# Moving tiles of a matmul kernel laid in a row and read in turns from neighbouring 16-byte lines

## The chip, the cores and the metric

The kernel runs on one core of a Trainium2 chip. The metric is the device time of one execution in microseconds (us). TensorE is called PE here (its weight loads PEld), VectorE DVE, ScalarE ACT, GpSimd POOL, and SyncE, which issues nearly all DMAs, SP.

## What is computed

One encoder layer on 1024 tokens of width 1024, all in float32: a SwiGLU block, a sub-layer that mixes tokens in two branches (retention and multi-scale pooling), a second SwiGLU block, and a last norm.

```python
h = x
h = h + 0.5 * swiglu_ffn(rmsnorm(h, norm_ffn1), ffn1_w_in, ffn1_w_out)      # D_FF 2816
u = rmsnorm(h, norm_mix)
q, k, v, g_ret, p, gates = jnp.split(u @ w_in, split_points, axis=-1)       # 7168 columns
q, k = rotary(q), rotary(k) * 256 ** -0.5                                   # 4 heads of 256
ret = retention(q, k, v)                  # chunks of 64 tokens, decay by head
ret = per_head_rms_norm(ret) * silu(g_ret)
pool_out = multiscale_pool(p, pool_w, pool_scale)   # windows of 2, 4, 8, 16 tokens
gate = sigmoid(gates + gate_bias)
merged = gate[0] * (ret @ w_ret_up) + gate[1] * (pool_out @ w_pool_up)
h = h + merged @ w_out
h = h + 0.5 * swiglu_ffn(rmsnorm(h, norm_ffn2), ffn2_w_in, ffn2_w_out)
out = rmsnorm(h, norm_final)
```

## The kernel before

**Matmuls.** Activations stand with features on the 128 partitions and tokens along the row. Each float32 operand is split in two parts, hi (rounded to the matmul's 32-bit type) and lo (what is left): `split` is a cast on ACT, written to hi, and a subtraction on DVE, written to lo (`split_scaled` does it with a factor). A product of two operands takes three matmuls, `mm3` (lines 203 to 205): hi by hi, hi by lo, lo by hi. One operand is stationary (128 x 128, loaded by PEld), the other moves past it, 512 columns at a time, and the sum stands in one of eight PSUM banks. A moving tile is made by `operand` (or `put`, in class `Next`, for the normed input of a stage), and a stationary one by `weights`.

**Stages.** Every large product is a Strassen-like scheme of seven half-size products. The input of a stage is recombined into the tiles R11, R12, R21, R22 and T1 to T4 (names n1, n2, ru, mg, n3 for the five stages that use `Next`), and the weights into L11, L12, S1 to S4. `strassen` accumulates a group's products in three banks (a, b, e), which ACT and DVE read out. `common` shares products of the last kind between two groups; its matmuls have 256 columns. The order of the stages: `ffn_in` (tiles a_), `ffn_out` (tiles b), the values `values` (tiles v), the other projections `project` (q, k, g, p, and t for the gates), retention with the pool's products between its steps (`Unit`, `pool`, `pool_up`), the branch projection (ru) and output projection (wo), then `ffn_in` again (c_) and `ffn_out` again (d). The last half of the second `ffn_out` makes the products with L22 with the weights moving (`near`, `far`), so that those outputs come by token.

**Order.** A Python generator gives steps (a preparation and a body); the body is run four steps later. Side work waits in a queue (`flow`) of which one or two pieces are placed after each step. A scheduler then sets each engine's order, and each engine works through its own in that order. Buffers come from pools with a fixed count: 28 tiles of 4 KB a partition (`mv`) for moving tiles, 9 (`t4`), 8 half-size ones (`c2`), and so on. A tile in such a pool can be written once the last reader of the one that had the buffer is done, a DMA to memory included.

**The moving tile's layout.** This is what the change is about. The tile holds even tokens and odd tokens apart, each with hi and lo, and the matmul reads it alternately from the two, so that the product's columns are in the order of the tokens:

```python
def rows(name):
    return sb.tile([P, 2, 2, HD], F32R, tag="mv", bufs=N_MV, name=name)   # parity, hi/lo, 256
def by_two(src):
    return src.rearrange("p (a b) -> p b a", b=2)      # every second element of the source
def moving(m, at=slice(None)):
    return [m[:, :, z, at].rearrange("p b a -> p a b") for z in range(2)]
```

Successive reads of a matmul are therefore 2 KB apart, to and fro, and the split that fills a tile reads its source with a step of two elements. The retention's tiles are not laid so (`straight`, read from start to end), nor are the operands of the small matmuls that spread a row over the partitions (n10b, n20b, fin0b).

Places in the program that the prediction uses: the square sums of a norm (`square`, ACT line 291, added on DVE line 292); the read-outs b, v, p7 in `strassen` (lines 514, 519, 536); the read-outs bd and dd in `ffn_out` (line 986) and the sums bacc, dacc (line 983); vp and vf, the read-outs in `values` (lines 1358, 1364); the gates (line 1227); fin0sum and fin0b, the statistics of the last norm.

Of the kernel before, what the change touches and what calls it, by code (L numbers as in the profile page):

```python
# [17 lines left out]
P = 128  # L18
# [72 lines left out]
def block_kernel(ctx: ExitStack, tc, x, x_tok, vecs, f1_in, f1_out, w_in, w_v, pool_w, w_ret, w_pool, w_o,  # L91
                 f2_in, f2_out, g_row, rope, decay, consts, out, out_tok):
# [29 lines left out]

    def moving(m, at=slice(None)):

        return [m[:, :, z, at].rearrange("p b a -> p a b") for z in range(2)]
# [43 lines left out]
    QUARTER = slice(0, P), slice(P, HD)  # L169
# [37 lines left out]
    def parts(m, at=slice(None)):  # L207
        return m[:, 0, at], m[:, 1, at]

# [66 lines left out]
    class Norm:  # L276


        def __init__(self, name):
            self.name, self.ssq, self.seen = name, None, set()  # L280

        def square(self, mt, tokens, src):
# [3 lines left out]
            if tokens.start not in self.seen:  # L286
                act(dst, src, AF.Square)
                self.seen.update(range(tokens.start, tokens.stop, HD))
            else:
                q = c2(f"{self.name}q{mt}_{tokens.start}")[:, : tokens.stop - tokens.start]  # L290
                act(q, src, AF.Square)
                tt(dst, dst, q, ADD)

    class Next(Norm):


# [13 lines left out]
        def put(self, n, i, src, by=None):  # L310
            m = rows(f"{self.name}{n}{i}")
            self.M[n, i] = m
            if by is None:
                split(lay(m, 0), lay(m, 1), by_two(src))
            else:
                split_scaled(lay(m, 0), lay(m, 1), by_two(src), by)
# [66 lines left out]
        def blocks(self, R, tags, over=False):  # L383
# [6 lines left out]
            def sums(z):  # L390
                for i in range(2):
                    m = self.M[R, 2 * i + z]
                    v = c2(f"{self.name}x{i}{z}").rearrange("p (b a) -> p b a", b=2)
                    tt(v, lay(m, 0).bitcast(F32), lay(m, 1).bitcast(F32), ADD)
                    x.update({(i, j, z): v[:, :, QUARTER[j]] for j in range(2)})

            def difference(n, z):
# [5 lines left out]
                if n not in left:  # L403
                    m, at = self.M[R, z], QUARTER[1]
                else:
                    tag, bufs = left[n]
                    if (R, n) not in self.made:

                        self.made[R, n] = sb.tile([P, 2, 2, HD], F32R, tag=tag, bufs=bufs, name=f"{self.name}{R}{n}")
                    m, at = self.made[R, n], QUARTER[z]  # L410
                self.Y[R, n, z] = moving(m, at)
                split(lay(m, 0, at), lay(m, 1, at), to)
# [10 lines left out]
        def block(self, R, n, z):  # L423
# [4 lines left out]
            return moving(self.operand(R, 2 * n[0] + z), QUARTER[n[1]])  # L428
# [7 lines left out]
        def stats(self, sums=None, between=()):  # L436
# [4 lines left out]
            def row(q):  # L441
                if not q:
                    self.row = t4(f"{self.name}rb")
                copy(half(self.row, q), spread(self.r_tok[:, 4 * q : 4 * q + 4], f"{self.name}{q}"))
# [410 lines left out]
    def ffn_out(nx, ops, ready, w, res, name, sink, end, last=None):  # L855
# [7 lines left out]
        def rows():  # L863

            t["rb"] = wide(f"{name}rb")
            act(t["rb"], nx.rms(), AF.Copy, scale=0.5)
# [84 lines left out]
        def p4(k):  # L951
            return both("L22", k, lambda z: w[z, :, 2 * H : 3 * H]), ahead.pop(k) if k in ahead else t4s(k)
# [3 lines left out]
        def step(n, f, k, where, start, after):  # L956
            o = {}

            def prep():
                L, X = f(k)  # L960
                o["w"] = weights(L, f"{name}{n}w{k}")
                o["m"] = X if len(X.shape) == 4 else operand(X, f"{name}{n}m{k}")
# [24 lines left out]

        def settle(mt, j, src=None):
# [3 lines left out]
            tt(q, q, old.pop((mt, j)), ADD)  # L992

        def done(mt, j, where, i, to=sink):
# [4 lines left out]
            def end():  # L999
                tt(q, old.pop((mt, j), q), d, ADD)  # L1000
# [139 lines left out]
    def ffn1():  # L1140
# [4 lines left out]
        yield from ffn_out(first, ops1, ops_done["a"], f1_out, x, "b", mix.quarter, end1)  # L1145
# [18 lines left out]
    def project(kind, n):  # L1164
# [60 lines left out]
        def gate(i):  # L1225
            z, mt = pair[i], 2 * n + i
            act(z, z, AF.Sigmoid, bias=vec[:, V_B0 + mt : V_B0 + mt + 1])
# [812 lines left out]
```

## Time and profile before

| | |
|---|---|
| median of 3 runs | 2112.47 us (2112.11 to 2117.91) |
| profiled execution: its time, its span | 2112.98 us, 2111.2 us |
| granted TensorE clock, mean over the span | 0.996 |
| matmuls, weight loads | 10798 each |
| busy: PE, PEld, DVE, ACT | 2058.6, 1817.2, 1909.9, 1167.1 us |
| DMA | 313.60 MB, mean 149 GB/s |

A matmul's listed duration runs from its start to the end of its result, so it overlaps the next one's; the distance of two starts tells what one costs. "Idle before" names, for a group of instructions, how long its engine stood still just before and who ended that. A window's row gives an engine's busy time in a stretch of the span, and the granted clock in it.

### The profile page before, as it was taken

What the parts mean: (1) busy time and instruction counts of PE and PEld (TensorE: products, weight loads), DVE (VectorE), ACT (ScalarE), POOL (GpSimd) and SP (SyncE); (2) the same over time, 40 slices, a digit from 0 to 9 for tenths busy, and PEclk for the clock granted to TensorE, in tenths of its full rate; (3) what the DMA queues carried; (4) which work ended last, traced back from release to release, by engine and by line L of the source; (5) the groups of instructions that cost most, each with busy time, mean ns of one, the idle gap of its engine ahead of it and who ended that gap; (6) DMA issues with size and microseconds to landing.
All of it is one profiled execution on the core that took longest, in us unless ns stands there. A gap on an engine that the chain in (4) does not pass through costs nothing. (4 is left out here: it accounts for less than half of the span.)

```text
span 2111.2 us, 30162 instructions
## 1 busy us (share of the span) xinstructions
PE 2058.6 (98%) x10798; PEld 1817.2 (86%) x10798; DVE 1909.9 (90%) x3352; ACT 1167.1 (55%) x2082; POOL 0.2 (0%) x4
## 2 busy tenths in 40 slices
PE   9999999999999999999999999999999999999998
PEld 7888988888878888889998998878789988888887
DVE  8899898998996799999988888999999989899996
ACT  8644444564855534445457753556645544456564
POOL 0000000000000000000000000000000000000000
PEclk9999999999999999999999999999999999999999
DMA  6332423585542433333336667624223242457642
GB/s 239 100 135 84 141 89 128 206 267 180 188 137 67 133 111 120 109 130 110 130 139 221 197 218 252 226 80 160 70 82 137 91 131 86 140 195 261 213 140 100
DMA packets 116646, 313.60 MB, mean 149 GB/s; under 512 B 13072, under 2 KB 17296, under 8 KB 116496
## 3 DMA queue, kind: packets, MB, share of 16 engines
q1 hardware_dynamic: 115920, 310.63, 43.9%
q8 instruction: 84, 1.38, 0.3%
q10 hardware_dynamic: 576, 1.05, 0.1%
q14 instruction: 66, 0.54, 0.1%
HBM read 220.93 MB, written 90.70 MB: 148 GB/s over the span
## 5 line engine op out<-in xcount | busy, mean ns | idle before, releaser
L204 PE MATMUL c_b<-n3T,c_wS 128*128 128x512 f32 x176 | 67.0, 381 | 0.0
L205 PE MATMUL c_b<-n3T,c_wS 128*128 128x512 f32 x176 | 66.8, 379 | 0.0
L203 PE MATMUL c_b<-n3T,c_wS 128*128 128x512 f32 x176 | 66.6, 380 | 0.2 <-ACT n3T L178 0.2
L203 PE MATMUL a_b<-n1T,a_wS 128*128 128x512 f32 x168 | 63.7, 379 | 0.0
L204 PE MATMUL a_b<-n1T,a_wS 128*128 128x512 f32 x168 | 63.7, 379 | 0.0
L205 PE MATMUL a_b<-n1T,a_wS 128*128 128x512 f32 x168 | 63.7, 379 | 0.0
L203 PE MATMUL c_a<-n3R,c_wL 128*128 128x512 f32 x112 | 43.9, 392 | 3.5 <-ACT c_b L514 3.5
L203 PE MATMUL a_a<-n1R,a_wL 128*128 128x512 f32 x120 | 45.6, 380 | 0.2 <-ACT a_b L514 0.2
L204 PE MATMUL a_a<-n1R,a_wL 128*128 128x512 f32 x120 | 45.5, 379 | 0.0
L205 PE MATMUL a_a<-n1R,a_wL 128*128 128x512 f32 x120 | 45.5, 379 | 0.0
L204 PE MATMUL c_a<-n3R,c_wL 128*128 128x512 f32 x112 | 43.6, 389 | 0.0
L205 PE MATMUL c_a<-n3R,c_wL 128*128 128x512 f32 x112 | 43.5, 388 | 0.0
L204 PEld LDWEIGHTS c_b<-n3T,c_wS 128*128 128x128 f32 x176 | 33.3, 189 | 5.2 <-DVE n3T L179 0.4
L203 PEld LDWEIGHTS c_b<-n3T,c_wS 128*128 128x128 f32 x176 | 33.2, 189 | 5.0 <-ACT n3T L178 0.6
L205 PEld LDWEIGHTS c_b<-n3T,c_wS 128*128 128x128 f32 x176 | 33.3, 189 | 4.6
L205 PEld LDWEIGHTS a_b<-n1T,a_wS 128*128 128x128 f32 x168 | 31.8, 189 | 4.5
L204 PEld LDWEIGHTS a_b<-n1T,a_wS 128*128 128x128 f32 x168 | 31.8, 189 | 4.3
L203 PEld LDWEIGHTS a_b<-n1T,a_wS 128*128 128x128 f32 x168 | 31.8, 189 | 4.3
L179 DVE TENSOR_TENSOR c_wS<-c_S,c_wS 128x512 fp32r<-128x512 f32 x46 | 32.1, 700 | 3.0 <-ACT c_wS L178 2.9
L178 ACT CAST c_wS<-c_S 128x512 fp32r<-128x512 f32 x46 | 27.8, 623 | 12.3 <-DVE c_S L477 7.8
L179 DVE TENSOR_TENSOR a_wS<-a_S,a_wS 128x512 fp32r<-128x512 f32 x45 | 31.3, 698 | 3.5 <-ACT a_wS L178 3.4
L203 PE MATMUL c_e<-n3T,c_wS 128*128 128x512 f32 x88 | 33.5, 380 | 0.0
(3385 smaller groups left out, 8275.0 us busy)
## 6 DMA issues: line engine op xcount, KB each, us to landing
c_ra<-in_f_in SPq DMA_DIRECT2D x22, 512.0 KB, 3.8
c_rb<-in_f_in SPq DMA_DIRECT2D x22, 512.0 KB, 3.7
a_ra<-in_f_in SPq DMA_DIRECT2D x21, 512.0 KB, 3.9
a_rb<-in_f_in SPq DMA_DIRECT2D x21, 512.0 KB, 4.3
t<-au SPq DMA_DIRECT2D x11, 512.0 KB, 2.9
b<-ag SPq DMA_DIRECT2D x11, 512.0 KB, 3.8
r<-au SPq DMA_DIRECT2D x11, 512.0 KB, 3.7
bra<-in_f_out SPq DMA_DIRECT2D x11, 512.0 KB, 5.8
```

Of the source, the lines that this page charges most:

```text
L178: copy(hi, src)
L179: tt(lo, src, hi.bitcast(F32), SUB)
L203: mm(dst, w[0], m[0], start=start, stop=False, skip_group_check=True)
L204: mm(dst, w[0], m[1], start=False, stop=False, skip_group_check=True)
L205: mm(dst, w[1], m[0], start=False, stop=stop, skip_group_check=True)
```

## The change

The moving tile becomes one row for hi and one for lo, in the order of the source; the parity halves are gone. The matmul reads eight elements as 0, 4, 1, 5, 2, 6, 3, 7, that is, alternately from two neighbouring lines of 16 bytes. The product's columns come out in that order, and the order is not put right at once: a stage's output is in turned order, the next one's in twice turned order, and after three products it is the natural one again. So q, k, p and the gates come out natural after three stages; at the places where tiles of different order meet, one of them is read in turns by ACT or DVE (squares of the norm, the row of the norm, gates, residuals of the second `ffn_out`, the fourth product's right side), or the host lays an input out in turns (`x_two`, `f2_far`, `w_v`, and the final output's rows). The core of the diff:

```diff
-    def rows(name):
-        return sb.tile([P, 2, 2, HD], F32R, tag="mv", bufs=N_MV, name=name)
-    def lay(m, z, at=slice(None)):
-        return m[:, :, z, at]
-    def by_two(src):
-        return src.rearrange("p (a b) -> p b a", b=2)
-    def moving(m, at=slice(None)):
-        return [m[:, :, z, at].rearrange("p b a -> p a b") for z in range(2)]
...
     def operand(src, name):
-        m = rows(name)
-        split(lay(m, 0), lay(m, 1), by_two(src))
-        return m
-    def straight(src, name):
         m = mv(name)
         split(m[:, 0], m[:, 1], src)
         return m
...
+    def in_turns(x):
+        return x.rearrange("p (o b a) -> p o a b", b=2, a=4)
+    def in_row(x):
+        return x.rearrange("p (o a b) -> p o a b", b=2, a=4)
+    def back(x):
+        return x.rearrange("p (o a b) -> p o b a", b=2, a=4)
+    def in_lines(x):
+        return x.rearrange("p (o b a) -> p o b a", b=2, a=4)
+    def moving(m, at=slice(None)):
+        return [in_turns(x) for x in parts(m, at)]
...
+        def squared(self, dst, src):
+            if self.turns:                       # the norms n2 and n3 (class Next)
+                dst, src = in_row(dst), in_turns(src)
+            act(dst, src, AF.Square)
...
         def near(k):
             def prep():
                 l, r = p4(k)
-                scale(r, r, 0)
+                c = c2(f"{name}p4r{k}")
+                tt(in_row(c), in_turns(r), in_row(half(t["rb"], 0)), MUL)
                 L[k], X[k] = operand(l, f"{name}p4w{k}"), mv(f"{name}p4m{k}")
-                split(X[k][:, 0], X[k][:, 1], r)
+                split(X[k][:, 0], X[k][:, 1], c)
...
         def gate(i):
-            z, mt = pair[i], 2 * n + i
-            act(z, z, AF.Sigmoid, bias=vec[:, V_B0 + mt : V_B0 + mt + 1])
-            load(gates[mt], z)
+            mt = 2 * n + i
+            for j in range(2):
+                z = c2(f"{name}z{i}{j}")
+                act(in_row(z), in_turns(half(pair[i], j)), AF.Sigmoid, bias=vec[:, V_B0 + mt : V_B0 + mt + 1])
+                load(half(gates[mt], j), z)
...
         def store(o, j, i, src):               # values: one DMA for 128 rows instead of two for 64
-            to = vs[2 * o + j].rearrange("(a b) (h t c) -> b t a h c", b=2, h=2, t=4)
-            for z in range(2):
-                load(to[i % 2, i // 2 * 2 + z], src[z * P // 2 : (z + 1) * P // 2].rearrange("p (h c) -> p h c", h=2))
+            to = vs[2 * o + j].rearrange("p (h t c) -> p h t c", h=2, t=4)
+            load(to[:, :, i], src.rearrange("p (h c) -> p h c", h=2))
...
                 for kt in range(2):            # pool: the tiles pl, read straight
                     for j in range(2):
-                        mm3(dst[j], parts(w[0], 2 * kt + i), moving(Mg[kt][j]), kt == 0, kt == 1)
+                        mm3(dst[j], parts(w[0], 2 * kt + i), parts(Mg[kt][j]), kt == 0, kt == 1)
...
-            load(r, vs[self.h // 2 * 2 + self.nh][:, self.h % 2 * S : (self.h % 2 + 1) * S])
+            rows = vs[self.h // 2 * 2 + self.nh][:, self.h % 2 * S : (self.h % 2 + 1) * S]
+            rows = rows.rearrange("(g b a) c -> b g a c", b=2, a=4)
+            for b in range(2):
+                load(r[b::2], rows[b])
```

Counted in the two programs: 358 splits of 512 columns (302 casts and 56 scaled ones, each with its DVE instruction) lose the step of two; 7716 matmuls of 512 columns and 2184 of 256 read in turns by lines (before 7812 and 2184 by halves), and 96 more read straight; 68 ACT and 27 DVE instructions now read in turns.

What a scheduler makes of it, at three places. First, DVE in the first `ffn_out`, around the read-out bd of the bank that PE needs for bp3m's matmuls (bp3m, bp4m: moving tiles; bp3w: stationary). Before:

```order
L179 TENSOR_TENSOR bp3w_5417<-bs_4073,bp3w_5417 128x512
L179 TENSOR_TENSOR bp3m_5506<-bR_5500,bp3m_5506 128x2x256
L179 TENSOR_TENSOR bp3m_5526<-bR_5500,bp3m_5526 128x2x256
L179 TENSOR_TENSOR bp4m_5532<-bT_5529,bp4m_5532 128x2x256
L179 TENSOR_TENSOR bp3w_5438<-bs_4182,bp3w_5438 128x512
L986 TENSOR_TENSOR bd_5447<-bp5a_5222,brb 128x512
```

After:

```order
L162 TENSOR_TENSOR bp3w_5417<-bs_4073,bp3w_5417 128x512
L162 TENSOR_TENSOR bp3m_5506<-bR_5500,bp3m_5506 128x512
L162 TENSOR_TENSOR bp3m_5526<-bR_5500,bp3m_5526 128x512
L162 TENSOR_TENSOR bp4m_5532<-bT_5529,bp4m_5532 128x512
L162 TENSOR_TENSOR bp3w_5438<-bs_4182,bp3w_5438 128x512
L993 TENSOR_TENSOR bd_5447<-bp5a_5222,brb 128x512
```

Nothing moved there; the moving tiles' instructions lost their two halves. Second, ACT in the projections, at the first gates (t0A, t0B: the two outputs of the group; p3b, t1b: read-outs that `strassen` needs; p3w, t1w: stationary tiles). Before:

```order
L1227 ACTIVATE t0A<-t0A,vec 128x1024
L514 COPY p3b<-p3a 128x512
L1241 COPY p1s_1_7388<-p1B 128x1
L1227 ACTIVATE t0B<-t0B,vec 128x1024
L514 COPY t1b<-t1a 128x512
L1250 COPY p1s_2_7341<-p1e_7361 128x16
```

After:

```order
L1246 ACTIVATE t0z_7443<-t0A,vec 128x512
L161 CAST t1wS_7426<-t1S_7424 128x512
L1246 ACTIVATE t0z_7446<-t0A,vec 128x512
L543 COPY p3p_7466<-p3e 128x512
L161 CAST p3wS_7450<-p3S_7351 128x512
L1246 ACTIVATE t0z_7468<-t0B,vec 128x512
L1246 ACTIVATE t0z_7471<-t0B,vec 128x512
L526 COPY p3v<-p3b 128x512
```

The gates stand some products later, behind p3b's read-out and ahead of p3v's, and in four instructions with tiles of their own. Third, DVE at the end of the second `ffn_out`, from the last read-outs dd to the statistics of the last norm (dT: the raw fourth operand; dp4m, dp4w: its parts and the weights'; n4ssq: the square sums). Before:

```order
L986 TENSOR_TENSOR dT_20205<-dT_20205,drb 128x512
L179 TENSOR_TENSOR dp4m_20189<-dT_20165,dp4m_20189 128x512
L179 TENSOR_TENSOR dp4w_20209<-dL_20202,dp4w_20209 128x2x256
L986 TENSOR_TENSOR dT_20205<-dT_20205,drb 128x512
L179 TENSOR_TENSOR dp4m_20212<-dT_20205,dp4m_20212 128x512
L179 TENSOR_TENSOR dp4w_20226<-dL_20202,dp4w_20226 128x2x256
L986 TENSOR_TENSOR dd_20061<-dp5a_19513,drb 128x512
```

After:

```order
L295 TENSOR_TENSOR n4ssq<-n4ssq,n4q_512_20174 128x512
L162 TENSOR_TENSOR dp4w_20179<-dL_20147,dp4w_20179 128x512
L162 TENSOR_TENSOR dp4m_20182<-dp4r_20177,dp4m_20182 128x512
L237 TENSOR_SCALAR fin0v<-fin0sum 128x4
L162 TENSOR_TENSOR dp4w_20233<-dL_20225,dp4w_20233 128x512
```

Before, the fourth operand is complete (but for one split) ahead of dd; after, its last six pieces come behind dd, four of them behind the statistics.

More of the change, by code (lines that the diff above doesn't have):

```diff
@@ L443, in row @@
                     self.row = t4(f"{self.name}rb")
-                copy(half(self.row, q), spread(self.r_tok[:, 4 * q : 4 * q + 4], f"{self.name}{q}"))
+                to, b = half(self.row, q), spread(self.r_tok[:, 4 * q : 4 * q + 4], f"{self.name}{q}")
+                if sums is not None:
+                    to, b = in_row(to), in_turns(b)
+                copy(to, b)
                 if q:
@@ L951, in p4 @@
         def p4(k):
-            return both("L22", k, lambda z: w[z, :, 2 * H : 3 * H]), ahead.pop(k) if k in ahead else t4s(k)
+            return both("L22", k, lambda z: beyond[z] if last else w[z, :, 2 * H : 3 * H]), ahead.pop(k) if k in ahead else t4s(k)
         bk = {}
@@ L986, in scale, with onto_old @@
             tt(q, src, half(t["rb"], j), MUL)
+        def onto_old(q, d, mt, j):
+            r = old.pop((mt, j), None)
+            if r is None:
+                tt(q, q, d, ADD)
+            elif last:
+                tt(in_lines(q), in_lines(d), back(r), ADD)
+            else:
+                tt(q, d, r, ADD)
         def settle(mt, j, src=None):
@@ L1320, in body @@
                 for i in range(4):
-                    mm3(bk[where, i], [m[:, i % 2, z, QUARTER[i // 2]] for z in range(2)], w, start and k == 0, k == 3)
+                    mm3(bk[where, i], parts(m, slice(i * P, (i + 1) * P)), w, start and k == 0, k == 3)
                     if k == 3:
@@ L1547, in values @@
         def values(self):
-            self.V = [straight(half(self.src["v"], n), f"v{self.name}{n}") for n in range(2)]
+            self.V = [operand(half(self.src["v"], n), f"v{self.name}{n}") for n in range(2)]
             if self.nh == 0:
```

72 lines of the change are left out of this document (39 added, 33 removed).

## The prediction

> **What bounds the kernel now.** First the page's busy line, then single matmuls in the timeline, then the list of who waited for whom.
>
> ```profile
> PE 2058.6 (98%) x10798; PEld 1817.2 (86%) x10798; DVE 1909.9 (90%) x3352; ACT 1167.1 (55%) x2082; POOL 0.2 (0%) x4
> ```
>
> PE is busy in 98% of the span, so there are two ways to a shorter time: matmuls that follow each other faster, or fewer of the some 50 us without a matmul. A matmul's listed duration overlaps the next one's; its price is the distance between two starts.
>
> ```profile
> 81.06 0.38 PE L204 MATMUL a_e<-n1T,a_wL 128*128 128x512 f32 x1
> 81.28 0.38 PE L205 MATMUL a_e<-n1T,a_wL 128*128 128x512 f32 x1
> 81.49 0.63 PE L273 MATMUL n10b<-n10dg,ones_r 128*128 128x512 f32 x2
> 81.96 0.38 PE L203 MATMUL a_b<-n1R,a_wS 128*128 128x512 f32 x1
> 82.17 0.38 PE L204 MATMUL a_b<-n1R,a_wS 128*128 128x512 f32 x1
> ```
>
> The first two and the last two read their moving tile alternately from two rows 2 KB apart (`moving`): 0.21 to 0.22 us from start to start. The pair in the middle reads a tile straight through: 81.49 to 81.96 is 0.47 us for two, 0.235 each. Reading in turns is worth some 0.016 us for 512 columns, and at 0.216 it leaves 2.4 columns a nanosecond. The change keeps reading in turns, at another distance; what that costs is the largest unknown here.
>
> The other way, the waits of PE:
>
> ```profile
> PE c_a L203 <- ACT c_b L514: 3.5, 1, 3.5
> PE c_x L203 <- ACT cg L601: 3.2, 6, 0.6
> PE vL L204 <- DVE vL11w L179: 2.6, 1, 2.6
> PE bp5a L203 <- DVE bd L986: 2.3, 1, 2.3
> PE fin0sum L255 <- DVE n4ssq L292: 2.1, 1, 2.1
> PE vS L203 <- ACT vf L1364: 2.0, 1, 2.0
> PE dp5a L203 <- DVE dd L986: 2.0, 1, 2.0
> PE wo1b L203 <- ACT wo1wS L178: 1.8, 1, 1.8
> PE bp6b L203 <- DVE bacc L983: 1.7, 2, 1.4
> PE dp6b L203 <- DVE dacc L983: 1.7, 2, 1.4
> PE vL L203 <- ACT vp L1358: 1.3, 1, 1.3
> PE wo0a L203 <- ACT wo0b L514: 1.3, 1, 1.3
> PE ru0a L203 <- ACT ru0b L514: 1.2, 1, 1.2
> ```
>
> They are many and short (a releaser, us in total, times, longest), at the joints of stages, where new moving operands are made. Do these joints hang on DVE's queue? In the stretches before five of them, DVE never rests (columns after the window: PE, PEld, DVE, ACT, POOL busy us):
>
> ```profile
> 550.70:559.70 9.00, 6.72 (x32) 5.57 (x31) 8.97 (x14) 7.23 (x12) 0.00 (x0) 1.00 0.77 244
> 586.00:623.20 37.20, 34.07 (x156) 28.58 (x154) 37.20 (x58) 22.45 (x31) 0.00 (x0) 1.00 0.40 129
> 1318.00:1335.20 17.20, 16.04 (x75) 13.72 (x73) 17.20 (x26) 16.07 (x22) 0.00 (x0) 1.00 0.59 202
> 1374.70:1422.10 47.40, 42.90 (x194) 35.66 (x192) 47.23 (x75) 24.56 (x40) 0.00 (x0) 1.00 0.27 89
> 2036.90:2043.90 7.00, 5.02 (x25) 4.09 (x23) 7.00 (x11) 6.55 (x10) 0.00 (x0) 1.00 0.70 228
> ```
>
> So there an instruction that is shorter on DVE brings everything behind it forward.
>
> **The change, part by part.** *Conversions into moving tiles.* A split is one ACT instruction (hi) and one DVE instruction (lo). Before, it reads every second element; after, straight. Rows of both kinds:
>
> ```profile
> L178 ACT CAST c_wS<-c_S 128x512 fp32r<-128x512 f32 x46 | 27.8, 623 | 12.3 <-DVE c_S L477 7.8 <-PE c_a L205 4.1 <-DVE c_S L494 0.4
> L178 ACT CAST bp6m<-br 128x512 fp32r<-128x512 f32 x11 | 9.7, 885 | 0.0
> L179 DVE TENSOR_TENSOR c_wS<-c_S,c_wS 128x512 fp32r<-128x512 f32 x46 | 32.1, 700 | 3.0 <-ACT c_wS L178 2.9
> L179 DVE TENSOR_TENSOR bp6m<-br,bp6m 128x512 fp32r<-128x512 f32 x11 | 9.3, 849 | 0.0
> ```
>
> The straight ones cost 623 and 700 ns, the others 885 and 849: 0.26 us less on ACT and 0.15 on DVE, for 358 splits of 512 columns (counted in the two programs): 93 us of ACT and 54 of DVE busy time. Nearly all of it lies beside matmuls and buys nothing. What counts is the splits in the queue ahead of a wait:
>
> ```profile
> L179 DVE TENSOR_TENSOR bp3m<-bR,bp3m 128x512 fp32r<-128x512 f32 x6 | 4.7, 843 | 0.0
> L179 DVE TENSOR_TENSOR bp4m<-bT,bp4m 128x512 fp32r<-128x512 f32 x2 | 1.5, 764 | 0.0
> L179 DVE TENSOR_TENSOR n2T<-bacc,n2T 128x512 fp32r<-128x512 f32 x7 | 5.6, 824 | 0.0
> L179 DVE TENSOR_TENSOR ruT<-ret,ruT 128x512 fp32r<-128x512 f32 x6 | 4.7, 834 | 0.0
> L179 DVE TENSOR_TENSOR mgT<-ru,mgT 128x512 fp32r<-128x512 f32 x6 | 4.8, 839 | 0.1
> L179 DVE TENSOR_TENSOR dp3m<-dR,dp3m 128x512 fp32r<-128x512 f32 x7 | 5.1, 781 | 0.0
> ```
>
> (each from the window of its place, in the order of the five windows.) Against 700 ns:
> - 559.7, bp5a: 6 x 0.143 + 2 x 0.064 = 1.0 us of the 2.3. A second piece hangs on it: the clock after the wait, below.
> - 623, vL: 18 such splits of four kinds stand in the 37 us (n2T's seven are shown) at some 0.13: 2.3, of which I take 2.0.
> - 1335, ru0a: 15 (six shown) at 0.13 make 1.9, more than the wait; the whole 1.2.
> - 1409 to 1426, wo0a, wo1b and their like: 23 splits at 0.12, 2.8.
> - 2043.9, dp5a: 7 x 0.081 = 0.6, and its clock.
> - bp6b and dp6b: three splits ahead of each, 0.8 together.
> - vL behind vp and vS behind vf: ACT's queue, about four splits of 0.26; 1.0.
> - All that is shorter (the first tiles, c_a, in whose way stand added instructions too): 1.0, between 0 and 3.
>
> After three of the longest waits the granted clock (the column behind POOL) is about half for some 3.5 us:
>
> ```profile
> 559.70:563.20 3.50, 3.50 (x9) 2.75 (x10) 3.50 (x7) 1.37 (x4) 0.00 (x0) 0.52 0.87 315
> 655.10:658.60 3.50, 3.50 (x9) 2.84 (x10) 1.90 (x3) 2.50 (x5) 0.00 (x0) 0.54 0.50 146
> 2044.00:2047.50 3.50, 3.50 (x10) 2.84 (x11) 3.50 (x7) 1.26 (x2) 0.00 (x0) 0.59 0.75 243
> ```
>
> Nine or ten matmuls where 16 would fit: 1.4 to 1.9 us lost. A wait of 2.0 us is followed by it, the 1.8 at wo1b isn't; a wait cut by half may not be. I count half of it at 559.7 and at 2043.9: 0.95 + 0.9. [...]
>
> Sum of gains: 1.95 + 2.0 + 1.2 + 2.8 + 1.5 + 0.8 + 1.0 + 1.0 = 12.3 us.
>
> [...]
>
> *The moving read.* 7716 matmuls of 512 columns and 2184 of 256 now hop 16 bytes to and fro instead of 2 KB. No row of before shows this pattern. From below: 0.216 us is the densest row there is, gain 0. From above: the straight read, 0.235. In both the old and the new pattern each line serves four of eight reads, in turns with one other; only the distance differs. So it is nearest to the old row, and I take 0. The upper end would be 7716 x 0.016 = 123 us.
>
> *Pool.* Its 96 matmuls now read straight:
>
> ```profile
> L203 PE MATMUL px<-pl,pw 128*128 128x512 f32 x32 | 12.5, 392 | 0.3 <-DVE g3A L1180 0.3
> ```
>
> 3 x 32 at 0.016: 1.5 us more, on the path, since PE is the bound.
>
> *Instructions that now reorder.* 32 squares, 32 gates and 4 others on ACT, 27 adds and products on DVE read in turns. No row has that; bounds are a straight row and an every-second row, so 0 to 0.26 us each on ACT and 0 to 0.15 on DVE; taken at the upper end, 18 us on an ACT with 45% idle and 4 us on DVE. Squares and residuals stand in the same queues that lose 93 and 54 us: 0.
>
> *Gates.* 16 sigmoids in place become 32 into tiles of the pool of eight (c2), each held until its store has landed:
>
> ```profile
> L1227 ACT ACTIVATE t0A<-t0A,vec x1: 1148/1148/1148, 779.6 to 779.6; 128x1024 f32<-128x1024 f32 x1
> DMA to landing us min/median/max: 2.6/2.6/2.6
> ```
>
> The second gate tile of a group reuses the first's buffer, so ACT may stand for up to 2.6 us, with PSUM copies behind it that PE awaits; SP issues 16 more stores, and 16 fewer for v. Eight groups: 0 to 8 x 1.3 = 10 us. Most copies have another group's matmuls ahead of PE; I take 1.0.
>
> *The end.* In the last stage products with L22 get a buffer of their own from that same pool, and DVE makes the last four pairs of them after fin0sum, not before; PE's n4s matmuls follow them closely to the end. DVE has there some 17 us of work for 77 matmuls (17 us): between -1 and +5, I take 1.5.
>
> Sum: -12.3 + 1.5 + 1.0 + 1.5 = -8.3. The profiled execution took 2112.98 us (span 2111.2), 0.5 above the median of 2112.47; so 2104.7 on its scale and **2104** on the median's.
>
> **The rivals.** (1) *Neighbouring lines are read worse than distant ones.* Every matmul pays; 1.1 ns more on each of 7716 (0.217 instead of 0.216) eats the whole gain, 1.9 ns makes it slower than the bound, and the straight rate gives 2104 + 123 = 2227, with as much again per column for those of 256. For it: no row shows the pattern; the pair at 81.49 proves that addresses matter. Against it: the old pattern changes line at every read too and is the fastest row. [...] Chance 0.13.
>
> (2) *Nothing reaches PE.* Many of the waits end with an ACT copy out of PSUM (c_a, c_x, vS: 8.7 us), which has no stride to lose. If only the waits that end with DVE shrink (vL, bp5a, dp5a, bp6b, dp6b: 2.0 + 1.0 + 0.6 + 0.8 = 4.4), the 4.0 of costs cancel them: 2112, no change. Against it: ACT's copy at 1335 itself waits in a joint where DVE is full. Chance 0.24.
>
> (3) *The pool of eight.* All 10 us of the gates, and 5 at the end, instead of 2.5: 2117; slower only with a second mishap. Chance 0.05.
>
> (4) The forecast's case, 2090 to 2106: 0.58.
>
> **How the numbers follow.** A change within 0.3%, 6.3 us, can't be told from none: faster means under 2106.1. Rivals 1 and 3 make slower 0.18, rival 2 makes same 0.24, the rest is faster. Low end: all DVE-ended waits of the joints gone and the three clock pieces with them, about 24 us: 2088. High end: rival 1 up to 3 ns a matmul, 2128; its rest is left out.
>
> **What would show it.** Starts of a_b matmuls 0.216 apart: the read costs nothing; px at 0.23: pool pays. ACT casts of bp6m near 623 and DVE's near 700: the split. DVE busy near 1860, ACT near 1090. Waits bp5a, vL and ru0a shorter and fewer stretches of half clock: the joints. t0z with a wait of ACT on a DMA, or new waits of PE on copies between 780 and 1040: rival 3. Wrong is the whole if the distance of starts is over 0.217, whatever DVE gains.

## The result, and the profile after

The changed kernel takes 2089.97 us (median of 4 runs, 2086.87 to 2090.97) against 2112.55 for the kernel before (median of 4 runs). The ratio of the two is 0.9885, with a 95% interval of 0.9866 to 0.9904. The change gains 22.6 us; the forecast, 2104, was a gain of 8.5. The profiled execution took 2086.87 us (span 2084.3), 3 us under its median, so the traces differ by 27 us, not 22.6.

The page's busy line, a split in the middle of ffn1 out (groups by line: busy us, mean ns, idle before), and matmuls in the timeline:

```profile
PE 2048.2 (98%) x10798; PEld 1812.0 (87%) x10798; DVE 1869.4 (90%) x3352; ACT 1100.8 (53%) x2098; POOL 0.2 (0%) x4
```
```profile
L162 DVE TENSOR_TENSOR bp6m<-br,bp6m 128x512 fp32r<-128x512 f32 x11 | 7.6, 691 | 0.0
L161 ACT CAST bp6m<-br 128x512 fp32r<-128x512 f32 x11 | 6.8, 615 | 0.0
```
```profile
80.62 0.38 PE L181 MATMUL a_b<-n1R,a_wS 128*128 128x512 f32 x1
80.83 0.38 PE L182 MATMUL a_b<-n1R,a_wS 128*128 128x512 f32 x1
81.05 0.38 PE L183 MATMUL a_b<-n1R,a_wS 128*128 128x512 f32 x1
```

The splits are as short as forecast (615 and 691 ns, from 885 and 849), DVE and ACT stand where they were forecast (1869 and 1101; 1860 and 1090), and matmuls still start 0.21 to 0.22 us apart. So both prices were right. Who PE waits for (releaser, us in total, times, longest):

```profile
PE c_x L181 <- ACT cg L608: 3.4, 6, 0.6
PE q1a L183 <- DVE q1wL L162: 3.2, 1, 3.2
PE a_x L181 <- ACT ag L608: 1.8, 4, 0.5
PE g2b L181 <- ACT g2ws L161: 1.7, 1, 1.7
PE wo1b L181 <- ACT wo1wS L161: 1.7, 1, 1.7
...
PE vL L182 <- DVE vL11w L162: 1.1, 1, 1.1
PE c_a L182 <- DVE n3R L166: 1.1, 2, 1.0
...
PE c_a L181 <- ACT c_b L521: 0.8, 1, 0.8
```

The waits at bp5a, bp6b, ru0a, wo0a, dp5a, dp6b and fin0sum are gone, vL's 2.6 us has become 1.1, and c_a's 3.5 us has become 1.1 and 0.8. New is q1a in the projections. The stretches of half clock behind bp5a and dp5a are gone too (columns as in the prediction; before, the clock there was 0.52 and 0.59, with 9 and 10 matmuls):

```profile
553.10:556.60 3.50, 3.50 (x18) 3.07 (x17) 3.50 (x7) 1.47 (x3) 0.00 (x0) 1.00 0.83 293
2019.00:2022.50 3.50, 3.50 (x18) 3.07 (x17) 3.50 (x7) 3.19 (x7) 0.00 (x0) 1.00 0.49 186
```

Length of each stage in us, worked out from the traces. A stage begins here with the same matmul in every run, the first one into a_a, bp1a, vL, k0a, ob, ru1a, wo1a, c_a or dp1a; some of these stand a few us behind the stage's true start, and ob some 15 us behind the retention's. The last stage ends with the last matmul. The last two columns are runs from below (t4_rows and d_gates):

| stage | before | after | layout undone | gates in place |
|---|---|---|---|---|
| start | 29.2 | 28.4 | 29.4 | 28.1 |
| ffn1 in | 380.2 | 379.4 | 380.1 | 378.7 |
| ffn1 out | 207.8 | 199.7 | 206.3 | 200.4 |
| values | 85.5 | 79.2 | 84.4 | 79.2 |
| projections | 446.1 | 452.7 | 457.6 | 442.9 |
| retention, pool | 182.5 | 183.2 | 182.5 | 182.3 |
| ru | 74.0 | 72.5 | 73.0 | 72.5 |
| wo | 78.5 | 73.6 | 79.3 | 73.6 |
| ffn2 in | 407.4 | 402.8 | 408.2 | 401.5 |
| ffn2 out | 214.0 | 205.3 | 211.8 | 205.4 |

Eight stages gained 35.7 us, and the projections and the retention lost 7.3; what follows the last matmul takes 6.0 us before and 7.6 after. Of the 35.7 us, some 28 are time in which PE stood still and some 7 are matmuls at half clock (worked out from the starts of the matmuls). The second part differs between executions: the other three runs of the changed kernel had a mean granted clock of 0.997 or 0.998, the profiled one 0.999.

The experiments ask what carried the gain and what cost the loss. c_both, a_dve, b_act, t4_rows, t2_hop1k, t6_rows_straight, a_hop, b_hop, d3_straightread and e_dist leave the order of PE's, DVE's and ACT's instructions as it is in the changed kernel; the others change it in places. Each time is compared with runs of the kernel before beside it, whose median moved between 2109.3 and 2114.0 from one set of runs to another; the ratio to it is given for that, with its 95% interval.

### The profile page after: what moved, and what is told of

Its sections match the earlier page's. It is cut to its first block, busy times and chain, and to the rows that moved or that the text cites. A ratio compares the mean times of both kernels' runs of the same rounds, so it can differ in the third digit from the quotient of the medians.

```text
span 2084.3 us, 30190 instructions
## 1 busy us (share of the span) xinstructions
PE 2048.2 (98%) x10798; PEld 1812.0 (87%) x10798; DVE 1869.4 (90%) x3352; ACT 1100.8 (53%) x2098; POOL 0.2 (0%) x4
## 4 chain that ended last, share of the span: by engine, by line
PE 74%; DVE 18%; issue 3%; ACT 3%; DMA 1%; SPq 0%; ACTq 0%; DVEq 0%
PE c_b L181 2%; PE c_b L182 2%; PE c_b L183 2%; PE a_b L181 2%; PE a_b L182 2%; PE a_b L183 2%; PE c_e L182 2%; PE c_e L183 2%; PE c_e L181 2%; PE a_e L181 2%; PE a_e L183 2%; PE a_e L182 2%; PE c_a L183 1%; PE c_a L182 1%; PE c_a L181 1%
## 5 line engine op out<-in xcount | busy, mean ns | idle before, releaser
L182 PE MATMUL c_e<-n3T,c_wL 128*128 128x512 f32 x88 | 33.5, 380 | 0.1
```

Source lines behind the costliest of these rows:

```text
L182: mm(dst, w[0], m[1], start=False, stop=False, skip_group_check=True)
```

## Experiments

### 1. The stride of the source, undone (c_both, a_dve, b_act)

```diff
     def split_m(hi, lo, src):                       # splits into moving tiles only
-        copy(hi, src)
-        tt(lo, src, hi, SUB)
+        copy(two_out(hi), two_in(src))              # two_in: "p (a b) -> p b a", every second element
+        tt(two_out(lo), two_in(src), two_out(hi), SUB)
```

(and the same in the scaled split; a_dve has the second line alone, b_act the first.)

> The changed kernel with one thing undone: the 358 splits into moving tiles read every second element of their source again, on ACT and on DVE, into the new tile; order of the instructions on every engine, gates, stores and moving reads stay as changed (the tokens of the result stand in another order). Theory 1, the splits carry the gain: the joints of the stages (bp6b, bp5a, vL, vS, ru0a, wo0a, c_a, dp6b, dp5a) get back their waits and three to five windows of half clock; the joints gained 37 us between the two traces, some 5 of them at the end of ffn2 out where the order changed too, so 2090 + 28 to 34 = 2118 to 2124. Theory 2, the new order of instructions and the fewer transfers of v carry it: under 2098, with the joints' waits as in the changed kernel.

> The changed kernel with only DVE's half of each split into a moving tile (lo) reading every second element again; ACT's half reads straight, so lo belongs to other tokens than hi and the result is not the reference's. Theory 1a, as the prediction had it, the joints hang on DVE's queue alone: at least four fifths of what undoing both gives, 2112 to 2124. Theory 1b, ACT's queue sets the joints: under 2098. Theory 1c, the two take turns (lo waits for hi): half of it, 2100 to 2110.

> The changed kernel with only ACT's half of each split into a moving tile (hi) reading every second element again; DVE's half reads straight, so lo belongs to other tokens than hi and the result is not the reference's. Theory 1a (DVE's queue alone): 2088 to 2094. Theory 1b (ACT's queue): 2112 to 2124. Theory 1c (in turns): 2100 to 2110.

Measured: c_both 2090.65 us (ratio 0.9906, 0.9892 to 0.9921), a_dve 2088.09 (0.9899), b_act 2088.98 (0.9901). Nothing came back that these intervals could tell from the changed kernel's. This doesn't show theory 2 to be right, for the rows show that the splits did not become long (groups by line of c_both):

```profile
L176 DVE TENSOR_TENSOR bp6m<-br,bp6m 128x512 fp32r<-128x512 f32 x11 | 7.5, 683 | 0.0
L175 ACT CAST bp6m<-br 128x512 fp32r<-128x512 f32 x11 | 7.3, 664 | 0.0
```

A source read at every second element costs DVE nothing here (683 against 691) and ACT 0.05 us (664 against 615). The same read cost 849 and 885 before, so something else in the old layout made it long. The runs on the two halves told nothing, since there was no length to divide.

### 2. The old layout piece by piece (t4_rows, t3_dst, t2_hop1k, t6_rows_straight)

```diff
     def moving(m, at=slice(None)):
-        return [in_turns(x) for x in parts(m, at)]                  # 16 bytes apart
+        return [in_rows(m, z).rearrange("p b a -> p a b") ...]      # t4, t6: rows 2 KB apart
+        return [x.rearrange("p (b a) -> p a b", b=2) ...]           # t2: 1 KB apart
     def split_m(m, src):
+        hi, lo = in_rows(m, 0), in_rows(m, 1)                       # t4, t3, t6: written in two rows
+        copy(hi, two_in(src))                                       # t6: the source straight, half by half
```

> The changed kernel, its order of instructions untouched, with the three things of the moving tiles undone together: a split reads every second element of its source, writes two rows 2 KB apart, and the matmuls read alternately from these rows (as before; the tokens of the result stand in another order, and the pieces of the products that are cut from a tile are of other tokens). The run that undid the source's stride alone stayed at 2090.7, with ACT's split at 0.66 us and DVE's at 0.68, so the 0.87 and 0.83 of before come from the destination or from the matmuls' reads. Theory L, the length of the splits carries the gain: 0.87 and 0.83 are back, and the time is 2115 to 2124 with the half-clock windows at the joints. Theory O, the order of the instructions and the transfers carry it: 2088 to 2095 although the splits are long again.

> As the run with the layout wholly undone, but the matmuls read as in the changed kernel, alternately from neighbouring 16-byte lines (what they read is half hi and half lo of other tokens, so the result is not the reference's, and PE waits for the lo of a tile where it waited for the hi; some 30 places change their order). Theory D, writing two rows 2 KB apart makes a split long: ACT 0.87, DVE 0.83 us; time 2115 to 2130. Theory R, the matmuls' reads of distant lines make it long: ACT 0.66, DVE 0.68; time 2090 to 2098, the later lo included.

> The changed kernel, order untouched, with splits that read every second element and write straight, and matmuls that read alternately from two places 1 KB apart in the row (the tokens of the result stand in another order). Distance between starts of matmuls 0.216 by both theories. Theory D (destination): splits at 0.66 and 0.68 us, 2088 to 2093. Theory R (the matmuls' reads of distant lines slow the other engines' accesses): splits at 0.8 to 0.87 and 0.8 to 0.84, squares and gates that read in turns longer too, 2110 to 2124.

> The changed kernel, order untouched, with the tiles and the matmuls' reads of before (two rows 2 KB apart), but splits that read their source straight, half by half (tokens as they come are not those of the reference). The prediction took the source's stride for what makes a split long; by that: ACT 0.62, DVE 0.70 us and a time of 2088 to 2092. Theory D (two rows as destination are slow by themselves): 0.87 and 0.83, 2115 to 2124. Theory R (reads of distant lines slow accesses that step over elements, and the source no longer does): 0.62 to 0.66 and 0.68 to 0.70, 2088 to 2092.

| run | source | tile written | matmuls read | us | ratio (95%) |
|---|---|---|---|---|---|
| t4_rows | every second | two rows | 2 KB apart | 2122.67 | 1.0049 (1.0037 to 1.0062) |
| t2_hop1k | every second | straight | 1 KB apart | 2120.88 | 1.0043 (1.0029 to 1.0056) |
| t3_dst | every second | two rows | 16 bytes apart | 2088.73 | 0.9889 (0.9875 to 0.9903) |
| t6_rows_straight | straight | two rows | 2 KB apart | 2089.60 | 0.9893 (0.9879 to 0.9906) |

The same groups, of t4_rows, t2_hop1k, t3_dst and t6_rows_straight in this order:

```profile
L187 ACT CAST bp6m<-br 128x512 fp32r<-128x512 f32 x11 | 9.9, 902 | 0.0
L188 DVE TENSOR_TENSOR bp6m<-br,bp6m 128x512 fp32r<-128x512 f32 x11 | 9.2, 841 | 0.0
```
```profile
L175 ACT CAST bp6m<-br 128x512 fp32r<-128x512 f32 x11 | 9.5, 867 | 0.0
L176 DVE TENSOR_TENSOR bp6m<-br,bp6m 128x512 fp32r<-128x512 f32 x11 | 9.2, 833 | 0.0
```
```profile
L188 DVE TENSOR_TENSOR bp6m<-br,bp6m 128x512 fp32r<-128x512 f32 x11 | 7.5, 680 | 0.0
L187 ACT CAST bp6m<-br 128x512 fp32r<-128x512 f32 x11 | 7.3, 665 | 0.0
```
```profile
L188 DVE TENSOR_TENSOR bp6m<-br,bp6m 128x512 fp32r<-128x512 f32 x11 | 7.5, 678 | 0.0
L187 ACT CAST bp6m<-br 128x512 fp32r<-128x512 f32 x11 | 6.8, 615 | 0.0
```

Theory R holds: in these runs a split is long only where its source is read at every second element **and** the matmuls beside it read from far apart. Either one alone costs at most 0.05 us, and writing the tile in two rows adds nothing (t3_dst against c_both). Theory L holds too: with the long splits back, 33 us come back (2122.67 against 2089.60 of the same set of runs). They come back in the stages that had gained and, with 4.9 us, in the projections (column "layout undone"), and with them many of the waits (list of t4_rows):

```profile
PE c_a L213 <- ACT c_b L553: 3.5, 1, 3.5
PE q1a L215 <- DVE q1wL L162: 3.2, 1, 3.2
...
PE vL L214 <- DVE vL11w L188: 2.6, 1, 2.6
PE vS L213 <- ACT vf L1413: 2.1, 1, 2.1
...
PE bp5a L213 <- DVE bd L1025: 1.8, 1, 1.8
```

t3_dst alone of these four changes PE's order, in some 35 places, because its hi and lo overlap; that cost nothing to be seen.

### 3. Which engine's half (a_hop, b_hop)

The edit of experiment 1 for one engine, in the kernel whose matmuls read 1 KB apart.

> The changed kernel, order untouched, with matmuls that read from two places 1 KB apart, and only DVE's half of each split (lo) reading every second element; ACT's half (hi) reads straight, so lo belongs to other tokens than hi and the result is not the reference's. With both halves long the time was 2120.9, with both short 2090.0: 31 us. DVE's half 0.82 us, ACT's 0.62. Theory 1a, as the prediction had it (the joints hang on DVE's queue): 2115 to 2121. Theory 1b (ACT's queue): 2088 to 2096. Theory 1c (in turns, since lo waits for hi): 2100 to 2110.

> The changed kernel, order untouched, with matmuls that read from two places 1 KB apart, and only ACT's half of each split (hi) reading every second element; DVE's half (lo) reads straight, so lo belongs to other tokens than hi and the result is not the reference's. ACT's half 0.86 us, DVE's 0.69. Theory 1a (DVE's queue): 2088 to 2096. Theory 1b (ACT's queue): 2115 to 2121. Theory 1c: 2100 to 2110.

Measured: DVE's half long 2112.93 us (ratio 0.9999, 0.9990 to 1.0008), ACT's half long 2103.40 (0.9954, 0.9941 to 0.9968). The long half of bp6m took 0.822 us on DVE and 0.879 on ACT, the other one 0.616 (ACT) and 0.686 (DVE). Against both short (t6_rows_straight, 0.9893) that is 0.0106 and 0.0061, some 22 and 13 us; both long (t2_hop1k, 1.0043) cost 32. Neither of the theories that name one engine holds; the third fits ACT's half, and DVE's lies between it and the first. Each half costs by itself, DVE's more, though its split grows by less (0.14 us against 0.26).

### 4. The gates (d_gates, d2_gates512, d3_straightread)

```diff
-            for j in range(2):
-                z = c2(f"{name}z{i}{j}")
-                act(in_row(z), in_turns(half(pair[i], j)), AF.Sigmoid, ...); load(half(gates[mt], j), z)
+            act(pair[i], pair[i], AF.Sigmoid, ...); load(gates[mt], pair[i])        # d_gates
+            z = half(pair[i], j); act(z, z, AF.Sigmoid, ...); load(..., z)          # d2_gates512, for j in 0, 1
+            act(z, half(pair[i], j), AF.Sigmoid, ...)                               # d3_straightread
```

> The changed kernel with the gates as before: 16 sigmoids of 1024 columns in place and one store each, not 32 of 512 columns read in turns into tiles of the pool of eight (the gates' tokens then stand in another order than the values they multiply). Theory 1, the gates cause what the projections lost between the two traces (9.8 us between 692 and 1134 us): 2077 to 2083, and the waits at q1a (3.2 us) and g2b (1.7) are gone. Theory 2, the matmuls only reach the projections earlier than DVE can have the operands, and the loss is the backlog: 2087 to 2092, with the same sum of waits in the projections.

> The changed kernel with the gates in 32 sigmoids of 512 columns and 32 stores, but in place and read straight, without tiles of the pool of eight (the gates' tokens then stand in another order than the values they multiply). With 16 sigmoids of 1024 in place the time was 2076.8, 13.2 under the changed kernel. Theory P, the pool of eight costs it: 2075 to 2080. Theory N, the number of sigmoids and stores costs it: 2086 to 2092.

> The changed kernel, order untouched, with the gates' sigmoids reading straight into the tiles of the pool of eight (the gates' tokens then stand in another order than the values they multiply). A sigmoid of 512 columns falls from about 0.8 us to 0.65, 32 times 0.15 = 5 us of ACT. Theory P (pool of eight, place in ACT's queue): 2087 to 2091. Theory I, the reading in turns makes ACT late: 2077 to 2084.

Measured: d_gates 2076.78 us (ratio 0.9843, 0.9829 to 0.9858), d2_gates512 2077.87 (0.9837, 0.9823 to 0.9850), d3_straightread 2086.49 (0.9874, 0.9860 to 0.9887). The kernels of the same set of runs as d_gates that kept the gates' tiles stand at 2088.1 to 2090.7, so these tiles cost about 12 us (9 to 13 by the ratios). It isn't the number of sigmoids or stores, for d2_gates512 has as many as the changed kernel. Between d2_gates512 and d3_straightread, of one set of runs, only the tiles differ and the order that follows from them: 8.6 us. That is the pool of eight and where it puts the sigmoids. What reading straight gives back, 2 to 3 us, lies within the intervals; a sigmoid of 512 columns took 0.84 us in turns and 0.72 straight. ACT's timeline of the changed kernel, then of d_gates, for the same group t4 (start, us, instruction, idle before):

```profile
926.81 0.84 ACT L1246 ACTIVATE t4z<-t4A,vec 128x512 f32<-128x512 f32 x1 [1.17 <-DVE q1B L1227]
928.81 0.62 ACT L161 CAST k1ws<-k1s 128x512 fp32r<-128x512 f32 x1 [1.16 <-DVE k1s L585]
929.34 0.83 ACT L1246 ACTIVATE t4z<-t4A,vec 128x512 f32<-128x512 f32 x1
...
931.99 1.57 ACT L1246 ACTIVATE t4z<-t4B,vec 128x512 f32<-128x512 f32 x2
...
935.16 0.63 ACT L161 CAST k1wx<-k1S 128x512 fp32r<-128x512 f32 x1
```
```profile
906.93 1.15 ACT L1244 ACTIVATE t4B<-t4B,vec 128x1024 f32<-128x1024 f32 x1
908.51 0.57 ACT L521 COPY k1b<-k1a 128x512 f32<-128x512 f32 x1 [0.43 <-PE k1a L183]
909.73 1.15 ACT L1244 ACTIVATE t4A<-t4A,vec 128x1024 f32<-128x1024 f32 x1 [0.64 <-DVE t4A L1204]
```

In place, the gates of t4 are done by 911. With tiles of the pool they are done some 17 us later, counted from ACT's copy k1b, which lies at 908.51 and 914.21: the first waits for DVE's rotation of q1 (line 1227), which reads a tile of that pool, and the four stand among the casts (k1ws, k1wx) of weights that PE needs next. PE's wait of 3.2 us at q1a is in the lists of the changed kernel and of d3_straightread, and in neither that of d_gates nor that of d2_gates512. Here the prediction's rival 3 shows with DVE as the one that holds the tiles, not the store. PE's queue also differs between d_gates and the changed kernel in some 30 places of the projections; how the 12 us divide between that order and the waits isn't separated.

### 5. The last products (f_near)

```diff
-                c = c2(f"{name}p4r{k}"); tt(in_row(c), in_turns(r), in_row(half(t["rb"], 0)), MUL)
+                scale(r, r, 0)
```

> The changed kernel with the last products' moving pieces scaled in place, read straight, without tiles of the pool of eight (their tokens then stand in another order than those they are multiplied with). The prediction put +1.5 us on the end for these tiles; by that 2087 to 2089. If they are free or help: 2090 to 2093.

Measured: 2090.78 us (2085.03 to 2095.06; ratio 0.9902, 0.9884 to 0.9920), which the changed kernel's 0.9885 doesn't differ from. In the traces ffn2 out takes 207.5 us, against 205.3, and what follows the last matmul 6.1 us, against 7.6; PE's order differs in 12 places near the end. So no cost of the tiles of the pool shows there, and the added 1.5 us isn't borne out.

### 6. How far is far (e_dist)

The kernel c_both with another distance in each stage: `in_turns(x, a)` with "p (o b a) -> p o a b" for a = 1 to 128 elements.

> The kernel whose splits read every second element (0.66 us on ACT with neighbouring lines, 0.86 with places 1 KB apart), order untouched, with another distance between the two places that the matmuls read in turns in each stage: 32 bytes in ffn1 in, 64 in ffn1 out, 16 in the values and projections, 128 in the pool's up-projection, 256 in ru, 512 in wo, 8 in ffn2 in, 4 (straight on) in ffn2 out (the tokens of the stages then don't fit each other). What is read: ACT's split by the stage that runs beside it, and the distance between starts of matmuls. Theory: only what shares or neighbours a 16-byte line is cheap, so 0.66 at 8 and 16 bytes and 0.86 from 32 bytes on, and starts at 0.216 for all but the straight read (0.227). Rival: the price grows with the distance.

ACT's splits, where matmuls of one distance alone ran beside them, took (median) 0.664 us for straight and 0.662 for 8 bytes, 0.665 for 16 and for 32, 0.672 for 64, 0.687 for 128, 0.879 for 256, 0.858 for 512; DVE's 0.68 to 0.69 up to 128 bytes, 0.865 at 256 and 0.834 at 512. Groups by line, the end of ffn1 in and ffn1 out (32 and 64 bytes, beside bp6m), the stretch of ru and wo (256 and 512, beside mgR and mgT), and ffn2 out (straight, beside dp5m):

```profile
L175 ACT CAST bp6m<-br 128x512 fp32r<-128x512 f32 x11 | 7.5, 680 | 0.0
```
```profile
L175 ACT CAST mgR<-ru 128x512 fp32r<-128x512 f32 x12 | 9.9, 856 | 2.8 <-PE ru3a L202 2.7
L175 ACT CAST mgT<-ru 128x512 fp32r<-128x512 f32 x12 | 9.8, 846 | 12.8 <-DVE ru L402 9.0 <-DVE ru L363 3.8
...
L175 ACT CAST dp5m<-dT 128x512 fp32r<-128x512 f32 x11 | 7.2, 659 | 1.5 <-DVE dp7w L162 1.5
```

The stage is not the reason: the casts mgR and mgT take 0.663 and 0.670 us in c_both, where the matmuls beside them read 16 bytes apart. Neither theory holds: the price neither starts beyond 16 bytes nor grows with distance; it steps between 128 and 256 bytes (0.687 to 0.879 us on ACT). Matmuls start 0.216 us apart for every distance of 16 bytes and more, and 0.227 for 8 bytes and for the straight read. (The kernel ran once, in 2118.44 us, 28 over c_both; some 2300 more matmuls at 0.227 make about 25 of them.)

### 7. Without the gates' tiles, and without any order to carry (g_c2, g_raw, n_lines)

g_c2 and g_raw keep the gates in place and reorder where DVE multiplies them in:

```diff
-                tt(h, in0, half(gt[which], n), MUL)
+                tt(in_row(h), in_row(in0), in_turns(half(gt[which], n)), MUL)
-                    tt(g, dst[j], g, MUL)                                            # pool_up
+                    h = c2(f"pz{mt}{j}"); tt(in_row(h), in_row(dst[j]), in_turns(g), MUL)   # g_raw: a raw tile
```

All three compute the layer. n_lines is the kernel before with the tile in a row: `by_two` reads "p (o a b) -> p o b a" (a = 4), the tile is written straight and read with `in_turns`, so products come out in order.

> A kernel that computes the reference: the changed one with the 16 gates in place and stored as they are, and the reordering moved to where a gate is multiplied in (DVE reads it in turns, and a product of the pool's side goes to a tile of the pool of eight). DVE's adds that read in turns took 0.695 to 0.71 us against 0.692 straight, so the reordering itself costs under 0.5 us in all. Theory: the 13.2 us that the gates' tiles cost in the projections come back and nothing is lost behind: 2077 to 2081. Rival: 16 tiles of the pool of eight are now held in the retention stage, as they were in the projections: 2083 to 2092.

> As the last, but the products of the pool's side go to tiles of the pool of four that holds raw weights, not to the pool of eight. Theory: 2077 to 2081. Rival: the weights of the pool's matmuls then load later, since four buffers serve two uses: over 2085, with PE waiting for pu weights.

> The kernel before with the moving tiles alone changed, and the tokens kept in their natural order through all stages: a split reads its source as 0,2,4,6,1,3,5,7 of every eight elements and writes straight, and the matmuls read the tile alternately from neighbouring 16-byte lines, so that each product comes out in order (values stored in the order of the tile and put right by their loads, as in the changed kernel; the 56 splits that also scale do so in two DVE instructions of 256 columns, some 0.2 us more each, 12 us of DVE). Gates, squares, row sums and the last products stay as before. Theory: what made the splits long is the distance between the places that the matmuls read, not the stride of the source; so ACT's split is at 0.66 to 0.80 us and DVE's at 0.69 without any order carried from stage to stage, the gates cost nothing, and the time is 2077 to 2086, under the changed kernel. Rival: a source that is read in turns of 8 bytes is as long as before on ACT (0.85 and more) and the doubled instructions fill DVE's queue at the joints: 2095 to 2112.

Measured: g_c2 2082.53 us (ratio 0.9858, 0.9842 to 0.9874), g_raw 2089.81 (0.9895, 0.9879 to 0.9911), n_lines 2085.66 (0.9864, 0.9840 to 0.9887). g_c2 ends between its theory and its rival: the projections take 445.6 us (452.7 in the changed kernel), but retention, ru and wo together 4.3 more than there. In g_raw the rival's time comes, with ru's weights in the place of the pool's. PE reaches ru1a 6.6 us earlier than in the changed kernel, but the load of the raw tile ru1rb is issued at 1319.1 us against 1319.5; PE waits for ru0wS, whose cast stands right behind that of ru1wS in ACT's queue (waits of PE),

```profile
PE ru0e L181 <- ACT ru0wS L161: 6.9, 1, 6.9
```

and ru takes 81.8 us instead of 72.5. n_lines has ACT's split at 0.667 us and DVE's at 0.693, and needs no reordered gates, squares or last products. So the gain never hung on the permuted order. g_c2 is 7 to 8 us under the runs beside it that keep the changed kernel's times (2089.8 and 2090.8), with an interval that doesn't touch f_near's; the changed kernel's own interval, of another set of runs, overlaps both g_c2's and n_lines'.

## Why the prediction was wrong

The time lies at the low end of the range, and the gain is 2.7 times the forecast. The mechanism, shorter splits and thereby shorter waits at the joints, was right in the main; two terms of the sum were mis-sized, the gains and the gates. By its own steps:

- **The price of a split** (0.26 us on ACT, 0.15 on DVE less): right as a number (885 to 615, 849 to 691), and the cause was half seen. The prediction took the source's stride for it; runs c_both, t6_rows_straight and e_dist show that the stride costs this only while matmuls read 256 bytes or more apart. Under near reads the step of two costs DVE nothing (683 against 691 ns, c_both against the changed kernel).
- **The moving read at 0**: right. 0.216 us, so rival 1 fell; e_dist has 0.216 for reads 16 bytes or more apart and 0.227 for 8 bytes and straight. Rival 2 fell too: of the waits that end with a copy on ACT, c_a's went from 3.5 us to 0.8 and vS's 2.0 is gone.
- **Sum of gains, 12.3 us**: the step that failed. Undoing the layout with all else equal costs 33 us (t4_rows against t6_rows_straight). Three parts of it were mis-sized. First, only DVE's saving was counted at the DVE-full joints, and too low: long splits on DVE alone cost some 22 us (a_hop) where 11.3 was counted, and on ACT alone some 13 (b_hop) where 1.0 was. Second, savings were counted only at named waits: ffn1 out gained 8.1 us, 6.5 of it time in which PE stood still (1.95 for bp5a and its clock and a share of 0.8 were counted), values 6.3 (3.0), wo 4.9 (2.8), ffn2 in 4.6 (some of the 1.0 for all that is shorter, c_a's 3.5 us wait among it). Third, the clock: before, five windows of half clock of 3.413 us lay inside the span, which cost some 7.4 us; 1.85 were counted. The profiled execution after has none there, but its other runs had a lower clock, so the part of the 22.6 us that is clock is open.
- **Pool, 1.5 us**: 96 matmuls at 0.227 instead of 0.216 make 1.1. Right in size, though its 0.016 us a matmul is less than its own pair gives (0.235 less 0.216 is 0.019) and more than what was measured (0.011).
- **Gates, 1.0 us**: about 12 measured. The bound of 10 us stood in the text and rival 3 named the pool, but the cost was put on a store that lands; the one wait of ACT in the rows above is for a tile held by DVE, and the gates' place in ACT's queue and PE's order changed with the tiles.
- **The end, +1.5**: no cost shows (f_near). From dp1a to the end of the span the trace has 212.9 us against 220.0.

So 33 and about 12 were measured where 12.3 and 1.0 had been put. The two errors partly cancelled, and that the time still lies inside the range is in part luck. t4_rows is 9.3 us over the kernel before, of which the gates are about 12; the other changes together then gain some 3 us, which no run separates.

## What to carry to other kernels

How long an instruction takes can depend on the address pattern of another engine's instructions beside it (here ACT's split of every second element: 0.664 us in c_both and 0.867 in t2_hop1k, which differ in how far apart PE's matmuls read): change either one alone before you pay for a reordering that changes both. Where an engine's queue is full ahead of many joints, count the saving of both engines of a chain and at every joint, unnamed ones too; the sum over the longest waits was a third of what came. And a tile added to a small shared pool is priced by who holds the other tiles and by what stands behind the new instruction in its queue, not by its own length.

## What the runs showed of the hardware that was not expected

**Length by distance.** ACT's and DVE's reads of 512 columns with a step of two elements take 0.86 to 0.90 and 0.82 to 0.87 us instead of 0.66 and 0.68 while PE's moving read goes to and fro over 256 bytes or more; at 128 bytes or less they take 0.66 to 0.69 and 0.68 to 0.69. Straight reads of the same size don't change with it (0.615 and 0.678 in t6_rows_straight, 0.615 and 0.691 in the changed kernel). Squares that read in turns of 16 bytes take ACT 0.75 us both in the changed kernel and in t2_hop1k, against 0.63 straight in the kernel before: their price is the same under near and far reads of PE. No run shows why the one read is lengthened and the others aren't.

**The clock's windows.** In every trace the half-clock stretches inside the span are whole numbers of 3.413 us, on one fixed grid for an execution (before: 3.412, 3.412, 6.826 and 3.413 us). The share of a window of that grid in which matmuls stream (worked out from their starts at 2.4 columns a nanosecond) told what followed. Over all 19 traces, up to the last matmul, all 37 windows at full clock with a share up to 0.33 were followed by half clock, 9 of the 20 between 0.34 and 0.40, and none above. So the same wait can cost or not. The wait of 3.2 us at q1a, in the changed kernel and in c_both, by windows of the grid:

```profile
871.10:874.50 3.40, 1.63 (x8) 1.09 (x6) 3.40 (x8) 0.41 (x1) 0.00 (x0) 1.00 0.34 131
874.50:877.90 3.40, 2.00 (x9) 1.78 (x10) 3.40 (x9) 0.88 (x3) 0.00 (x0) 1.00 0.01 2
```
```profile
874.20:877.60 3.40, 0.68 (x3) 0.63 (x4) 3.40 (x8) 0.44 (x2) 0.00 (x0) 1.00 0.00 0
877.60:881.00 3.40, 3.40 (x10) 2.68 (x9) 3.40 (x8) 0.81 (x3) 0.00 (x0) 0.50 0.01 2
```

In the first it falls across two windows and the clock stays at 1.00; in the second it fills most of one (0.17 streaming), and the next runs at 0.50. The prediction's reading, that half clock follows a wait of 2.0 us and not one of 1.8, was too simple. Nor need a window be idle: one with matmuls streaming for up to 0.33 of its length sufficed.
